# Input projection as a stage of its own, and attention moved beside the blocks that follow it

## The chip, the cores and the metric

The kernel runs on one core of a Trainium2 chip. The metric is the device time of one execution in microseconds. The kernel before takes 2442.66 us (median of 3 runs, 2442.2 to 2445.62). One further execution was profiled. The figures of the profile come from that one.

## The reference

One encoder layer, 512 tokens, width 2048, all in float32:

```python
h  = rmsnorm(x, norm_mix)
qa, ka, va, qb, kb, vb, ga, gb = split(h @ w_in)      # 1024|256|256|1024|1024|1024|2048|2048 columns
qa = rope(rmsnorm(qa)); ka = rope(rmsnorm(ka))        # 8 query heads, 2 key/value heads of 128
out_a = window_attention(qa, ka, va, sink)            # keys within 128 tokens, a sink logit per head
qb = rmsnorm(qb); kb = rmsnorm(kb)                    # 8 heads
out_b = neighbourhood_attention(qb, kb, vb, rpb)      # 8 x 16 window on a grid 64 wide, 2-D bias
merged = sigmoid(ga) * (out_a @ w_branch_a) + sigmoid(gb) * (out_b @ w_branch_b)
x = x + merged @ w_out
u = conv3(rmsnorm(x, norm_ffn) @ w_up) + conv_b       # 2 x 5632 columns, depthwise over tokens
x = x + (silu(gate) * val) @ w_down                   # gate, val = halves of u
```

The input projection `w_in` has 8704 columns: 17 blocks of 512.

## The kernel before

Every matrix product is made in three matmuls: each operand is split into a rounded part `hi` and a rest `lo` (`nc.scalar.copy` to the reduced type, then a subtraction on VectorE), and hi x hi, hi x lo and lo x hi are added up in PSUM. Weights are split in the kernel too, unit by unit, just before use. A unit is two 128-row tiles by 512 columns of a weight (512 KB); a block of `w_in` is 8 units.

A block runs in one of two ways:

- **Plain** (`step` and `run_step`, L120 and L220): four PSUM banks, 16 tiles of the inner dimension, three matmuls of 512 moving columns each, 192 in all. The weights are `Plain` units (their own pool `wst`) or, later on, `Tiles` units (pool `f` for the raw weights, pool `w` for the split ones).
- **As seven products** (`products`, L719): a two-by-two scheme after Strassen and Winograd. Units, activations and results are taken as 2 x 2 blocks of (128 rows, 256 columns); seven block products replace eight. It needs sums of weight blocks (`Product.sums`, three VectorE additions per unit, L632), sums of activations (`form_sums`, `forms`) and, once per block, `combine` (L816), which puts seven PSUM banks together into the result. 8 units x 7 x 2 x 3 = 336 matmuls of 256 moving columns.

For some `Product` units (`kept`) the sums are made long in advance: `make_early` (L680) fetches the weight on the POOL queue, adds (L651, four VectorE additions), stores the sums to DRAM, and the unit later loads them. `windows` says in which units that goes on.

The order of the program up to the branches: `kv_a` (L589) and `q_a` project the rows of branch a, plainly, `v_b` and `kq_b` those of branch b. Each of these steps puts the work that follows on a queue: `rows_of` (norm and rotary of 128 tokens), `head` (transposing a head on TensorE), `run` (one head's attention; `attention_out`, its second half, runs behind the next head). `run_step` takes `rate` entries from that queue per unit, with a raised priority of 400 instructions, so that attention's small matmuls, its VectorE and ScalarE work run between the plain matmuls. Then come the gates: three blocks plainly, five as products (L995 to L1003). `end_attention` (L858) runs what is left in the queue and closes the attention's pools just before the third. While that block runs, `form_h` loads `x` again and makes the forms of `h` for the products. After that `branch` a, `branch` b, the output projection, the up projection with its convolution, and the down projection.

A planner arranges the program of each engine: it simulates the kernel, and takes of the instructions that are ready the one with the highest priority. Instructions marked with `keep`, and every DMA on the SP queue (`dma`, L74), stay in the order in which they were written. Pools are stretches of on-chip memory; a tile over a closed pool waits for the tiles that lay there. `prep_to` splits the weights up to two units ahead, `advance` also loads up to four units ahead.

## Time and profile before

| what | value |
|---|---|
| runs, median (range) | 2442.66 us (2442.2 to 2445.62) |
| profiled execution | 2443.0 us |
| its span, first to last instruction | 2441.2 us, granted clock 0.998 |
| TensorE, VectorE, ScalarE, GpSimd busy | 99%, 77%, 52%, 13% |
| DMA | 517.63 MB in the span, mean 212 GB/s |
| transposes of heads and attention on TensorE | 64.0 to 531.0 us |
| first and last matmul | 5.3 and 2434.1 us |

In the tables of stretches a row gives start and end, the length, then for each engine its busy time and in brackets its instructions, then the granted TensorE clock (1.00 is full speed), the mean busy share of the 16 DMA engines and GB/s. In the groups a row gives line, engine, operation, tiles written and read, shapes, count, then busy time and mean ns of one, then the idle time ahead of them with what ended it. PEld is TensorE's loading of weights, which overlaps its matmuls.

### The profile page before, as it was taken

How to read it: one execution, taken by the hardware profiler on the slowest of the kernel's cores; microseconds unless marked ns; L12 is line 12 of the kernel's file. 1: busy time of each engine (PE TensorE's matmuls, PEld its weight loads, DVE VectorE, ACT ScalarE, POOL GpSimd, SP SyncE). 2: the span in 40 equal slices, each digit the busy share in tenths (PEclk: the TensorE clock that was granted, in tenths of full speed). 3: DMA queues.
4: the chain of work that ended last, by engine and by line, in shares of the span. 5: the costliest groups of instructions: out<-in, count | busy, mean ns of one | idle time of the engine just before them, and what ended most of it. 6: DMA issues, size and time to landing. Idle time of an engine off the chain costs nothing. (4 is left out here: it accounts for less than half of the span.)

```text
span 2441.2 us, 45026 instructions
## 1 busy us (share of the span) xinstructions
PE 2422.1 (99%) x17346; PEld 2264.5 (93%) x17346; DVE 1881.9 (77%) x2911; ACT 1280.2 (52%) x1862; POOL 314.1 (13%) x394
## 2 busy tenths in 40 slices
PE   9999999999999999999999999999999999999998
PEld 7888888888999888888999999999999999999998
DVE  6788676635788657555888888888888877888897
ACT  5254554544545323334566665756667566464643
POOL 1413233100000111110010111101111011000000
PEclk9999999999999999999999999999999999999999
DMA  5677777545455587664577877878778799675953
GB/s 195 243 244 242 255 254 266 174 141 192 169 178 169 194 285 228 237 241 165 161 203 211 221 209 210 219 211 222 208 211 216 213 268 266 172 250 134 315 167 126
DMA packets 300681, 517.63 MB, mean 212 GB/s; under 512 B 26160, under 2 KB 163120, under 8 KB 300464
## 3 DMA queue, kind: packets, MB, share of 16 engines
q1 hardware_dynamic: 217008, 318.18, 40.5%
q0 software_dynamic: 47168, 124.71, 21.0%
q10 hardware_dynamic: 36288, 71.84, 7.8%
q8 instruction: 136, 2.23, 0.4%
q14 instruction: 81, 0.66, 0.1%
HBM read 374.22 MB, written 94.37 MB: 192 GB/s over the span
## 5 line engine op out<-in xcount | busy, mean ns | idle before, releaser
L78 PE MATMUL mm<-s,wh 128*128 128x256 f32 (+1 forms) x9564 | 1689.4, 289 | 6.7 <-ACT wh L674 3.8
L78 PEld LDWEIGHTS mm<-s,wh 128*128 128x128 f32 x9564 | 1400.3, 188 | 48.7 <-ACT wh L674 5.1
L78 PE MATMUL mm<-s,wl 128*128 128x256 f32 (+1 forms) x4782 | 1184.1, 288 | 0.0
L78 PEld LDWEIGHTS mm<-s,wl 128*128 128x128 f32 x4782 | 817.6, 188 | 20.0
L674 ACT CAST wh<-f 128x1024 fp32r<-128x1024 f32 x594 | 547.7, 941 | 517.3 <-PE mm L78 400.1
L675 DVE TENSOR_TENSOR wl<-f,wh 128x1024 fp32r<-128x1024 f32 x594 | 642.8, 1087 | 171.1 <-ACT wh L674 161.6
L632 DVE TENSOR_TENSOR f<-f 128x256 f32<-128x256 f32 (+1 forms) x639 | 325.4, 509 | 7.6 <-DMA f<-in_w_down 2.3
L78 PE MATMUL mm<-hi,s 128*128 128x512 f32 x896 | 286.5, 395 | 5.3 <-ACT hi L162 5.3
L163 DVE TENSOR_TENSOR lo<-raw,hi 128x1024 fp32r<-128x1024 f32 (+1 forms) x97 | 117.7, 1213 | 122.5 <-ACT hi L162 116.8
L78 PEld LDWEIGHTS mm<-hi,s 128*128 128x128 f32 x896 | 168.4, 189 | 38.4 <-ACT hi L162 5.2
L78 PE MATMUL mm<-s,hi 128*128 128x512 f32 x640 | 195.3, 392 | 0.0
L776 DVE TENSOR_TENSOR wl<-f,wh 128x1024 fp32r<-128x1024 f32 x71 | 87.0, 1225 | 134.8 <-ACT wh L775 131.6
L162 ACT CAST hi<-raw 128x1024 fp32r<-128x1024 f32 (+1 forms) x97 | 101.0, 1041 | 155.0 <-PE mm L78 146.5
L775 ACT CAST wh<-f 128x1024 fp32r<-128x1024 f32 x71 | 74.4, 1048 | 199.0 <-PE mm L78 185.4
L78 PE MATMUL mm<-lo,s 128*128 128x512 f32 x448 | 176.1, 394 | 0.0
L78 PEld LDWEIGHTS mm<-s,hi 128*128 128x128 f32 x640 | 119.5, 188 | 23.9
L1072 POOL DMA_DIRECT2D o<-a x44 | 52.9, 1202 | 584.5 <-ACT a L1071 517.6
L78 PE MATMUL mm<-s,lo 128*128 128x512 f32 x320 | 120.4, 392 | 0.0
L651 DVE TENSOR_TENSOR s<-s 128x256 f32<-128x256 f32 x236 | 97.6, 419 | 5.9 <-DMA s<-in_w_in 3.5
L78 PEld LDWEIGHTS mm<-lo,s 128*128 128x128 f32 x448 | 84.8, 189 | 16.1
L1069 ACT ACTIVATE o<-u,smalls 128x512 f32<-128x512 f32 x88 | 71.2, 809 | 18.8 <-ACT wh L674 13.8
L1080 POOL DMA_DIRECT2D o<-a x44 | 52.8, 1201 | 175.5 <-ACT a L1078 161.6
(156 smaller groups left out, 1825.1 us busy)
## 6 DMA issues: line engine op xcount, KB each, us to landing
f<-in_w_up SPq DMA_DIRECT2D x301, 256.0 KB, 3.7
o<-a POOLq DMA_DIRECT2D x88, 511.0 KB, 7.3
f<-sums SPq DMA_DIRECT2D x84, 512.0 KB, 5.6
f<-in_w_down SPq DMA_DIRECT2D x145, 256.0 KB, 4.2
raw<-in_w_in SPq DMA_DIRECT2D x63, 512.0 KB, 3.6
sums<-s ACTq DMA_DIRECT2D x118, 256.0 KB, 2.8
s<-in_w_up POOLq DMA_DIRECT2D x86, 256.0 KB, 5.5
s<-act SPq DMA_DIRECT2D x73, 256.0 KB, 6.1
```

The lines of the kernel that those rows point to most:

```text
L78: return nc.tensor.matmul(o, l, r, start=start, stop=stop, skip_group_check=True).ins
L162: nc.scalar.copy(hi[:, c:c + n], self.raw[:, c:c + n])
L163: nc.vector.tensor_tensor(lo[:, c:c + n], self.raw[:, c:c + n], hi[:, c:c + n].bitcast(F32), ALU.subtract)
L632: add = lambda *args: keep(nc.vector.tensor_tensor(*args, ALU.add))
L651: add = lambda *args: keep(nc.vector.tensor_tensor(*args, ALU.add))
L674: keep(nc.scalar.copy(hi, f))
L675: keep(nc.vector.tensor_tensor(lo, f, hi.bitcast(F32), ALU.subtract))
L775: keep(nc.scalar.copy(hi, self.f))
L776: keep(nc.vector.tensor_tensor(lo, self.f, hi.bitcast(F32), ALU.subtract))
L1069: keep(nc.scalar.activation(self.o[:, m], u[:, m], AF.Identity, bias=cb[:, i:i + 1], scale=cw[:, i, 1:2]))
L1072: keep(nc.gpsimd.dma_start(self.o[:, :, 1:], first[:, :, :S - 1], accum_op=ALU.add))
L1080: keep(nc.gpsimd.dma_start(self.o[:, :, :S - 1], third[:, :, 1:], accum_op=ALU.add))
```

## The change

The input projection of everything but branch b's queries and keys now comes first, without attention beside it:

1. `project_v`, two plain blocks with the values of branch b; their results go to DRAM (`raw_v`). The forms of `h` are made beside the second, from the `x` tiles that are still there.
2. Eight gate blocks and the three blocks of branch a's rows, all eleven as seven products. For the latter the operands are exchanged (`layout="t"`), so that results come out with tokens on partitions; they go to DRAM (`raw_a`).
3. Four plain blocks `project_b` with branch b's queries and keys (their rows go to DRAM too, `raw_b`), and then branch a's projection. All attention is queued in this stage, at 1.85 entries per unit in place of 1.25. Entries that need a raw row (`Loaded`) load it on the SP queue when they are among the first three of the queue. `end_attention` comes ahead of the last unit of branch a's third block.

The stages share on-chip memory: pools are opened and closed at their bounds (`begin_rows`, `begin_attention`, `end_attention`). All units are now `Tiles` or `Product` units with one common loading order (`ready`, `load_units`). The split weights of plain units and of the products' first part stay in one pool (`wa`) throughout. Sums made in advance are now kept for no gate unit, and for one unit of an up block in place of two; the down projection keeps its 17.

The core of the diff ("..." marks what is left out):

```diff
-N_SLOTS, N_P, N_TR, AHEAD = 56, 8, 4, 400
+N_SLOTS, N_EXTRA, N_P, N_TR, N_QR, AHEAD = 56, 8, 8, 4, 7, 400
...
-ATTENTION_RATE, RATE = 1.25, 3
+RATE, ATTENTION_RATE, LOOK = 1, 1.85, 3
...
+    ffn["f"], ffn["bufs"], ffn["width"] = open_("loads", "f1", side="right"), 4, 7
+    ffn["ahead"], ffn["limit"] = 1, -1
+    extra = open_("loads", "extra", side="right")
+    att = {}
+    first_banks = pool("pmm", 4, space=PSUM)
+    more_banks = open_("inner", "pmm1", space=PSUM)
+    banks = {"mm": deque([first_banks] * 4 + [more_banks] * 4)}
 
     def slot(dt=F32):
...
+    def ready(phase, d):
+        while at[phase] < len(units) and at[phase] <= min(at["use"] + d, ffn["limit"]):
+            at[phase] += 1
+            yield units[at[phase] - 1]
+
+    def load_units(d):
+        for u in ready("load", d):
+            u.load()
     def prep_to(n, hooks=((), (), ()), **kw):
...
-            u.prep(*hooks, **kw)
+        for i in range(at["prep"], min(n, ffn["limit"]) + 1):
+            load_units(i - at["use"])
...
     def run_queued(n):
         with tc.high_priority(offset=AHEAD):
             for _ in range(min(n, len(queue))):
+                for work in list(queue)[:LOOK]:
+                    if isinstance(work, Loaded):
+                        work.load()
                 queue.popleft()()
 
...
+    class Loaded:
+
+
+        def __init__(self, load, work, *args):
+            self.start, self.work, self.args, self.tile = load, work, args, None
+
+        def load(self):
+            if self.tile is None:
+                self.tile = self.start()
+
+        def __call__(self):
+            self.load()
+            self.work(self.tile, *self.args)
+
...
+    def load_row(src):
+        raw = att["rows"].tile([P, 4, HD], F32, tag="qr", name="qr", bufs=N_QR)
+        dma(raw.rearrange("p h d -> p (h d)"), src)
+        return raw
...
+        def rows_of(raw, t):
+            if on_row:
+                on_row(t, raw)
+            head_square(raw, nh, t, sums, HD if scaled else 1.0, g is not None)
...
+        queue.extend(Loaded(partial(load_row, src[:, t]), rows_of, t) for t in range(NT))
+        queue.extend(partial(head, h) for h in range(nh))
         return res
...
+    def project_v(half, **kw):
...
+            if m % 2 == 0:
+                held["v"] = quad("u")
+            nc.scalar.copy(held["v"][:, m % 2], ps)
+            if m % 2:
+                nc.gpsimd.dma_start(raw_v[2 * half + m // 2], held["v"])
+
+        step("f", w_in, [(C_VB + half * S, S)], hT, evac, **kw)
+
+    def project_b(pair, **kw):
+
+        def evac(t, ps):
+            o = att["heads"].tile([P, S], F32, tag="o", name="o", bufs=2)
+            nc.scalar.activation(o, ps, AF.Copy, scale=rows["rs"][:, t:t + 1])
+            nc.scalar.dma_start(raw_b[pair][:, t], o)
+
+        step("t", w_in, [(C_QB + pair * 256, 256), (C_KB + pair * 256, 256)], hT, evac,
+             post=lambda: heads_b(pair), rate=ATTENTION_RATE, **kw)
+
+    def heads_b(pair):
+        v = [None] * 2
+
+        def head_v(raw, h):
...
+                nc.tensor.transpose(b[:, i * P:(i + 1) * P], vt[:, k0:k0 + P], ident)
+            v[h] = split(b)
...
+        queue.extend(
+            Loaded(partial(load_row, raw_v[pair][:, h]), head_v, h) for h in range(2))
         res = row_heads(
...
+            raw_b[pair], 4, None,
+            lambda tiles, h: heads_T(tiles, h, part["gqb" if h < 2 else "gkb"], grid=True))
+        queue.extend(partial(run, i) for i in range(2))
+
+    def heads_a():
...
+            split_rows(vh[-1][:, half], vl[-1][:, half],
+                       raw[:, 2:].rearrange("p h d -> p (h d)"), rows["rs"][:, t:t + 1])
+
+        k = row_heads(raw_a[0], 2, "gka", heads_T, on_row=row_v)
+        for half in range(2):
+            scaled = []
+            q = row_heads(raw_a[1 + half], 4, "gqa", heads_T, scaled=scaled)
+
+            def run(i, half=half, q=q, scaled=scaled):
+                behind(attention_a(half * 4 + i, q[i], k, (vh, vl), scaled[0][:, :, i]))
+
+            queue.extend(partial(run, i) for i in range(4))
 
     pending = []
 
...
             added.append((e, u))
-        if early and any(a <= u < b - 4 for a, b in windows) and not (wide and u % 2):
+        if early and any(a <= u < b - 4 and u % n for a, b, n in windows):
...
+                        lh, ll, rh, rl = (
+                            (wh[:, s], wl[:, s], ah, al) if layout == "f" else
+                            (ah[:, s], al[:, s], wh, wl))
+                        mm(o, lh, rh, i == m == 0, False)
+                        mm(o, lh, rl, False, False)
+                        last["pe"] = mm(o, ll, rh, False, i == n - 1 and m == 1)
...
+    def begin_rows():
+
+        opened["loads"].close()
+        ffn["f"], ffn["bufs"], ffn["width"] = open_("rest", "f2", side="right"), 3, 4
+        ffn["ahead"], ffn["limit"] = 3, stage_ends[1]
+        att["tmp"] = open_("rest", "tmp2", side="right")
+        att["rows"] = open_("rest", "rows", side="right")
+        load_masks()
+        prep_to(at["use"] + 1)
+        load_units(2)
+        heads_a()
+
+    def begin_attention():
+
+        opened["inner"].close()
+        del ffn["q"], ffn["b"]
+        tmp["p"], tmp["n"] = att["tmp"], 4
+        att["heads"] = open_("rest", "heads", side="right")
+        att["p"] = open_("rest", "p", side="right")
+        banks["mm"] = deque([first_banks])
+        banks["tr"] = deque([open_("rest", "ptr", space=PSUM)])
+
     def end_attention():
         run_queued(len(queue))
         behind()
...
+        opened["rest"].close()
+        again = lambda name, **kw: ctx.enter_context(
+            tc.tile_pool(name=name, bufs=1, reuse_waits="tile", **kw))
+        ffn["f"], ffn["bufs"], ffn["width"] = again("f3", side="right"), 4, 7
+        ffn["ahead"], ffn["limit"] = 4, len(units) - 1
+        ffn["q"] = again("q3", side="right")
+        ffn["b"] = again("wb3")
+        tmp["p"], tmp["n"] = again("tmp3", side="right"), 3
         del banks["tr"]
...
+        load_units(2)
 
...
+    def form_h(j):
+
+        a, b = xt[2 * j], xt[2 * j + 1]
+        for i, x in enumerate((a, b)):
+            nc.scalar.activation(x, x, AF.Copy, scale=gmix[:, 2 * j + i:2 * j + i + 1])
+        left, right = slice(0, 256), slice(256, 512)
+        add = nc.vector.tensor_tensor
+        add(b[:, right], b[:, right], a[:, right], ALU.subtract)
+        add(a[:, right], a[:, left], a[:, right], ALU.subtract)
+        add(a[:, left], a[:, left], b[:, right], ALU.add)
+        add(b[:, left], a[:, left], b[:, left], ALU.subtract)
+        highs, lows = ((sums_slot(j), sums_slot(j)) for _ in range(2))
+        for hi, lo, x in zip(highs, lows, (a, b)):
+            nc.scalar.copy(hi, x)
+            add(lo, x, hi.bitcast(F32), ALU.subtract)
+        half = lambda k, c: (hT[2 * j + k][0][:, c], hT[2 * j + k][1][:, c])
+        both = lambda i, c: (highs[i][:, c], lows[i][:, c])
+        hf.append([half(0, left), half(1, left), both(1, left), both(0, right),
+                   both(1, right), both(0, left), half(1, right)])
...
+    def row_products(i, c, **kw):
+
+        def evac(*halves):
+            for h, u in enumerate(halves):
+                dst = raw_a[i][:, :, h * 256:(h + 1) * 256].rearrange("p (t m) n -> p m t n", m=2)
+                src = u.rearrange("p m (t n) -> p m t n", t=2)
+                for m in range(2):
+                    nc.gpsimd.dma_start(dst[:, m], src[:, m])
+
+        products(columns(c), range(KD // 2), hf, evac, layout="t", **kw)
 
...
+    def branch_a(blk):
+        def before(kb):
+            if kb == 1:
+                for m in range(4 * blk, 4 * blk + 4):
+                    ra[m] = slot()
+                    nc.gpsimd.dma_start(ra[m], gate_a[m // 2][:, m % 2])
+            if blk == 2 and kb == 3:
+                end_attention()
+            if blk == 3:
+                parts_behind(out_b, ob, 0)(kb)
+
+        def evac(o, ps):
+            m = 4 * blk + o
+            nc.vector.tensor_tensor(ra[m], ps, ra[m], ALU.mult)
+
+        step("f", w_branch_a, [(blk * 512, 512)], oa, evac, nk=8, before=before,
+             rate=ATTENTION_RATE)
+
...
+    project_v(0, pre=first_loads, before=split_hT)
+    project_v(1, before=form_h)
+    for blk in range(8):
+        gate_products(blk)
+    for i, c in enumerate((C_KVA, C_QA, C_QA + 512)):
+        row_products(i, c, after=(
+            lambda u: begin_rows() if u == 7 else None) if i == 2 else None)
+    stage_ends.append(len(units) - 1)
+    windows.append((len(units) + 1, len(units) + 44, 2))
+    for pair in range(4):
+        project_b(pair, pre=begin_attention if pair == 0 else None,
+                  before=parts_behind(out_a, oa, 2) if pair == 3 else None)
     for blk in range(4):
-        branch(w_branch_a, blk, oa, gate_a, evac_a, before=parts_behind(out_b, ob, 0))
+        branch_a(blk)
+    stage_ends.append(len(units) - 5)
+    windows.append((len(units) - 2, len(units) + 48, 3))
     for blk in range(4):
-        branch(w_branch_b, blk, ob, gate_b, evac_b)
+        branch_b(blk)
...
         view = w_up.rearrange("(d b p) (h n) -> d p b h n", b=2, p=P, h=2)
         products(view[:, :, :, :, s * 256:(s + 1) * 256], range(KD // 2), h2, evac,
                  before=before, after=after,
-                 kept={0: range(8), pairs_ff - 1: (2, 3, 7)}.get(s, (2, 3)))
+                 kept={0: range(8), pairs_ff - 1: (2, 3, 7)}.get(s, (2,)))
```

376 lines of the change are left out of this document (120 added, 256 removed).

## The prediction

> **What bounds the kernel now.** I read the page's span and busy lines first, then the waits of TensorE, then stretches of the span in which one kind of work runs alone.
>
> ```profile
> span 2441.2 us, 45026 instructions
> PE 2422.1 (99%) x17346; PEld 2264.5 (93%) x17346; DVE 1881.9 (77%) x2911; ACT 1280.2 (52%) x1862; POOL 314.1 (13%) x394
> ...
> L78 PEld LDWEIGHTS mm<-s,wh 128*128 128x128 f32 x9564 | 1400.3, 188 | 48.7 <-ACT wh L674 5.1
> ...
> PE mm L78 <- ACT hi L162: 5.3, 1, 5.3
> PE mm L78 <- ACT wh L674: 3.8, 1, 3.8
> PE mm L78 <- DVE s L1113: 1.5, 2, 1.2
> PE mm L78 <- ACT s L1112: 1.2, 1, 1.2
> ```
>
> TensorE is busy for 99% of the span and waits for others only 11.8 us in all (last four rows: total, times, longest; the row above them is the weight loads, with busy time and mean ns). 5.3 us of that is the start. A matmul that is gone is therefore worth its full spacing, as long as the other engines keep up. The spacing is read from stretches with one shape only (columns: length, busy time and count of PE, PEld, DVE, ACT, POOL, clock, DMA share, GB/s): branch projections with 512 moving columns in the first row, seven-product blocks with 256 columns in the others (gates, up projection, down projection).
>
> ```profile
> 840.00:1110.00 270.00, 270.00 (x1193) 223.58 (x1192) 158.11 (x249) 80.14 (x104) 34.75 (x62) 1.00 0.72 242
> 680.00:800.00 120.00, 120.00 (x1059) 120.00 (x1058) 99.02 (x136) 60.25 (x72) 3.21 (x6) 1.00 0.53 171
> 1300.00:1900.00 600.00, 599.86 (x5278) 599.47 (x5277) 527.27 (x722) 386.20 (x506) 76.86 (x64) 1.00 0.81 215
> 2300.00:2400.00 100.00, 100.00 (x883) 100.00 (x882) 91.33 (x139) 46.16 (x57) 4.37 (x8) 1.00 0.53 171
> ```
>
> 270/1193 is 0.2263 us for a 512-column matmul, and 120/1059 is 0.1133 us for one of 256. The clock is 1.00 throughout, and no stretch is held back by the DMA engines or VectorE, although VectorE is already at 83, 88 and 91% beside the products.
>
> **The matmuls that go.** A plain 512-column block of the input projection has 4 outputs x 16 tiles x 3 = 192 matmuls: 192 x 0.2263 = 43.4 us. As seven products it has 8 units x 7 x 2 x 3 = 336 of half the width: 336 x 0.1133 = 38.1 us. Five blocks already run as products, and eleven will, so six are converted: 6 x 5.4 = **-32.3 us**. The two `v` blocks and the four `q`/`k` blocks of branch b stay plain, and nothing else is taken from TensorE.
>
> [...]
>
> **VectorE beside the products.** These rows price one unit (busy time, mean ns).
>
> ```profile
> L675 DVE TENSOR_TENSOR wl<-f,wh 128x1024 fp32r<-128x1024 f32 x182 | 222.4, 1222 | 80.0 <-ACT wh L674 80.0
> L675 DVE TENSOR_TENSOR wl<-f,wh 128x768 fp32r<-128x768 f32 x182 | 173.3, 952 | 24.3 <-ACT wh L674 24.3
> L632 DVE TENSOR_TENSOR f<-f 128x256 f32<-128x256 f32 x262 | 110.3, 421 | 3.2
> L632 DVE TENSOR_TENSOR f<-f 128x512 f32<-128x512 f32 x130 | 89.1, 685 | 0.0
> ...
> L823 DVE TENSOR_TENSOR u<-mm,t 128x512 f32<-128x512 f32 x46 | 31.6, 688 | 4.4 <-ACT t L827 2.1 <-DVE t L823 0.5
> L823 DVE TENSOR_TENSOR u<-t,u 128x1024 f32<-128x1024 f32 x23 | 28.0, 1219 | 0.1
> ...
> L845 DVE SCALAR_TENSOR_TENSOR t<-mm,t 128x512 f32<-128x512 f32 x23 | 15.7, 681 | 0.0
> ```
>
> Sums of weights made in advance and kept in DRAM fall, by the lists of kept units in the code, from 84 (16 for gates, 51 for the up and 17 for the down projection) to 48: no gate unit has them and an up block has one in place of two. A unit without them adds 0.685 + 2 x 0.421 = 1.53 us to VectorE. A gate block today spends 0.825 x 38.1 = 31.4 us there with two units kept; with none it is 34.5 of 38.1 us, 91%. An up block goes from 33.5 to 35.0 us, 92%. The down stretch above holds full spacing at 91%, so I cost this at **0**. What hides it is the matmuls of the unit in flight; if nothing above those 91% were usable, an up block would be up to 0.3 us over, +6 in 21 blocks. Below zero it can't go, since those stretches have no stall to give back. The row products have no row factor (1.219 us x 2 less), so they are lighter than the gates. The new `form_h` runs beside the second plain `v` block: 4 x 0.42 + 2 x 0.69 = 3.1 us a unit plus a 1.22 us weight split against 24 x 0.2263 = 5.4 us, so it is covered.
>
> **The seams between stages.** Today plain blocks hand over to products once, at 617 us:
>
> ```profile
> 620.86 3.10 PE L78 MATMUL mm<-s,wh 128*128 128x256 f32 x14 [3.82 <-ACT wh L674]
> ...
> 616.00:636.00 20.00, 16.18 (x122) 15.68 (x121) 17.65 (x30) 13.54 (x25) 3.07 (x5) 0.91 0.67 249
> ```
>
> TensorE stands 3.82 us and then runs at a reduced clock: four wide and 118 narrow matmuls need 14.3 us at full spacing, the stretch took 20, so the seam costs **5.7 us**. The cause is that the weight pool of the plain blocks must close first. In the change that pool (`wa`) is never closed, so this seam should go. A new one appears after the last row product: `begin_rows` may prepare the first unit of `project_b` only after that block's `combine`, whose last VectorE steps need the last matmul: 0.681 + 1.219 us, then the new unit's split of about 1.22 us, 3.1 us in which TensorE has nothing but one matmul. I take the new seam to cost as much as the old one, net **0**, with bounds from -5.7 (it is hidden) to +6 (the old one stays too).
>
> [...]
>
> The second seam is `end_attention` inside branch a's third block: loads of the next block go into tiles over the old `f2`, scratch and mask tiles, so unit 0 of block 3 is loaded one unit ahead and not two. The load takes 3.6 us and the two splits 1.0 and 1.2 (rows below), 5.8 against 5.4 us of cover. I take **+2**, between 0 and +10.
>
> **The attention beside less work.** Attention now runs beside 12 plain blocks. Afterwards it has 43 units of 24 matmuls (four blocks, and branch a up to unit 3 of its third block). Rows: all engines from 50 to 540 us, then in the same stretch VectorE's weight splits (L163), its sums in advance (L651), ScalarE's weight casts (L162) and TensorE's attention instructions, and last the densest 100 us.
>
> ```profile
> 50.00:540.00 490.00, 489.97 (x2456) 415.54 (x2455) 341.17 (x697) 233.08 (x445) 127.86 (x169) 1.00 0.67 223
> ...
> 50.00:540.00 490.00, 90.59 (x74) 1.00 0.67 223
> ...
> 50.00:540.00 490.00, 97.62 (x236) 1.00 0.67 223
> ...
> 50.00:540.00 490.00, 77.75 (x74) 1.00 0.67 223
> ...
> 50.00:540.00 490.00, 100.47 (x672) 91.37 (x672) 76.93 (x138) 55.22 (x91) 1.00 0.67 223
> ...
> 100.00:200.00 100.00, 99.97 (x489) 84.26 (x488) 84.85 (x179) 42.90 (x87) 38.82 (x39) 1.00 0.68 229
> ```
>
> - TensorE: 2456 - 672 = 1784 plain matmuls x 0.2263 = 404 us, so attention itself takes 86 us of it. New stage: 43 x 24 x 0.2263 + 86 = 320 us.
> - VectorE: 341 - 91 - 98 = 153 us for attention, plus 43 splits x 1.22 = 53, plus about 20 sets of sums at 1.65 us (98 us for 236 additions, four a set) = 33 (the window now fetches every second unit), plus 16 splits and evacuations of branch a at 0.69 = 11: 250 of 320 us, 78%.
> - ScalarE: 233 - 78 = 155, plus 43 x 1.05 = 45, plus 5: 205 us, 64%.
>
> From 100 to 200 us VectorE ran at 85% with TensorE at 99.97 busy, so 78% should fit. I cost the crowding at **+3**, nearest to that row. Ends: 0, and, if VectorE can do no more than its mean share of today (341/490 = 70%), 250/0.70 - 320 = +37.
>
> **Raw rows through DRAM.** 36 rows of 256 KB are stored and read back through SP's queue.
>
> ```profile
> raw<-in_w_in SPq DMA_DIRECT2D x63, 512.0 KB, 3.6
> f<-sums SPq DMA_DIRECT2D x84, 512.0 KB, 5.6
> sums<-s ACTq DMA_DIRECT2D x118, 256.0 KB, 2.8
> s<-act SPq DMA_DIRECT2D x73, 256.0 KB, 6.1
> ...
> SPq L75 <- DVE lo L163: 168.7, 32, 10.3
> ```
>
> A row needs about 2.8 us to be stored and up to 6.1 us to come back. A row is asked for two queue entries before its use (`LOOK` 3), two entries are 2/1.85 units, about 6 us, and its store lies far earlier, except in the first unit. Bytes: 36 x 0.5 MB more, but 36 kept sums fewer, each 512 KB fetched, 512 stored and 512 loaded in place of 256. Cost **0**. If the cover goes, a late row delays attention, which the crowding's bound already holds. One wait is new: `project_b` empties its four banks on ScalarE through two `o` tiles, which attention's results use as well, so the third bank waits for the store of the first, some 2.8 us. Behind that copy stand weight casts and attention on ScalarE, and behind the bank the next block's matmuls. The first bank is complete 18 matmuls (4.1 us) before the block's end and the third is wanted 12 matmuls (2.7 us) after it, so the store is covered by 4 us. I take **+1**, between 0 and four times 2.8 us.
>
> **Sum.** 2441.2 - 32.3 + 0 + 0 + 2 + 3 + 0 + 1 = 2414.9 us of span. The profiled execution took 2443.0 us, 1.8 more than its span, and the runs' median of 2442.66 lies 0.3 below it: 2414.9 + 1.8 - 0.3 = **2416 us**. Start, the stall when the down projection begins (L1112, L1113) and the tail are untouched.
>
> **The rivals.**
> - *More than forecast.* The new seam is hidden and nothing crowds: 2416 - 5.7 - 6 = 2404. For it: the stage's VectorE share is only 78%. Against: `combine` is ordered ahead of the new unit.
> - *VectorE sets the attention stage.* Branch a's rotary work comes first and bunches up. At 74%, midway between the mean share and what is needed, 250/0.74 = 338, 18 us over: 2416 - 3 + 18 = 2431. Against it stands the 100 to 200 us row; for it, that this was 100 us and now 320 are wanted.
> - *SP's queue turns on the kernel (slower).* A row load takes one of seven row tiles and waits for it, and each weight load issued later stands behind it. SP's tile waits reach 10.3 us today without touching TensorE, because loads run ahead. With three weight tiles a load is issued two units before its split, 10.9 us less 3.6 of transfer, some 7 us of slack. There are six changes of row group (one `k`/`v`, two `q`, four `b`). If attention runs late by more than the slack, each overshoot stops TensorE. Beyond (32.3 + 4.9)/6, about 6 us each, the kernel is slower by over 0.2%; at 8 us it is 2410 + 48 = 2458 (2410 is the sum without its 6 us of stalls). Against it: rows of a group are freed by its head transposes, and two attention heads are queued after them.
> - *Weight loads set the spacing.* If a narrow matmul had to wait for its own weight load, 188 ns by the first fence, a product block would take 336 x 0.188 = 63 us, 20 over a plain one: 2416 + 32 + 120 = 2568. The loads overlap each other in the product rows (1058 in 120 us), which denies it. [...]
> - *Nothing moves.* Crowding near the end of its range eats the gain: 2410 + 32 = 2442.
>
> **How the numbers follow.** Chances: forecast (2409 to 2422) 0.52; more than forecast 0.12; VectorE sets the stage (2422 to 2437) 0.17; nothing moves 0.07; SP's queue 0.11; weight loads 0.01. A measurement of this kernel tells about 0.2%, 4.9 us, from no change. Faster: 0.52 + 0.12 + 0.17 = 0.81; same 0.07; slower 0.12. The likeliest case's own range is 2409 to 2422. The range for 8 in 10 reaches from 2402 (seam gone, no crowding, 2 us for the clock) to 2440, which takes in the VectorE rival and leaves out the slower ones.
>
> **What would show it.** Right: 6 x 336 = 2016 more narrow matmuls and 6 x 192 = 1152 fewer wide ones, with about 880 in each 100 us of the gate stage; one stall of 3 to 4 us before the first `project_b` matmul, and none at the first gate block; VectorE near 91% beside the gates and 78% in the attention stage. Wrong: TensorE waits spread through the attention stage for weight casts or attention tiles (VectorE rival), or SP waiting on row tiles just before weight loads that TensorE then waits for (SP rival), or clearly fewer than the 5278 matmuls that 600 us of the up projection hold now.

## The result, and the profile after

The changed kernel takes 2517.56 us (median of 4 runs, 2513.09 to 2520.27) against 2442.88 us for the kernel before on the same chip: a ratio of 1.0302, interval 1.0283 to 1.0320. It is 3% slower, where 1% faster was forecast. The profiled execution took 2513.09 us, with a span of 2510.9 us.

The head of the page of the changed kernel:

```profile
span 2510.9 us, 46821 instructions
...
PE 2433.6 (97%) x18210; PEld 2297.7 (92%) x18210; DVE 1995.6 (79%) x3065; ACT 1318.6 (53%) x1883; POOL 270.0 (11%) x334
```

There are 864 matmul records more, as 2016 narrow ones for 1152 wide ones must give. TensorE now stands idle for 77 us of its span (2510.9 - 2433.6); before it was 19. Four stretches of the changed kernel (columns as in the prediction's rows): gates and row products; the attention stage, from the first matmul of `project_b` to the unit behind `end_attention`; branch b with the output projection; the up projection.

```profile
100.00:535.00 435.00, 428.65 (x3700) 426.66 (x3699) 358.81 (x512) 196.69 (x227) 14.58 (x25) 1.00 0.41 134
...
535.40:938.90 403.50, 354.70 (x1721) 291.11 (x1721) 261.27 (x531) 199.17 (x412) 83.97 (x110) 0.95 0.55 183
...
980.00:1300.00 320.00, 320.00 (x1747) 278.15 (x1746) 225.68 (x381) 131.87 (x198) 45.56 (x75) 1.00 0.72 236
1340.00:2040.00 700.00, 696.24 (x6084) 692.71 (x6083) 631.34 (x886) 445.12 (x580) 86.62 (x73) 1.00 0.77 202
```

The attention stage is where the time went: 403.5 us for 44 units, where the prediction's 320 us for 43 units make 325. TensorE is busy for 88% of it at a clock of 0.95, while VectorE is busy for only 65% and ScalarE for 49%. No engine is full.

To place the rest, I compared the time between the starts of successive matmuls with full spacing (0.227 us for 512 columns, 0.175 for 384, 0.113 for 256, 0.108 for a transpose). Full spacing alone fell from 2405.0 to 2371.9 us, by 33.1. What lies above it rose from 23.7 to 126.2 us. A gap is a matmul that starts more than 0.26 us late, a short delay one that starts 0.08 to 0.26 us late:

| stretch of the changed kernel | gaps, us | short delays, us | rest, us |
|---|---|---|---|
| 0 to 100 us, start and `v` blocks | 3.7 | 2.6 | 0.4 |
| 100 to 535, gates and row products | 7.8 (9 gaps) | 1.0 | 6.8 |
| 535 to 980, attention stage | 60.8 (60 gaps) | 24.3 | 0.7 |
| 980 to the end | 10.0 (21 gaps) | 2.9 | 4.6 |

The expectations below call the short delays "lowered clock" or "slow clock". That is true of part of them only: in the attention stage about 13.5 of the 24.3 us lie in the eight stretches, 41 us in all, in which the granted clock was 0.50. The other 11 us came at full clock. Before, attention's stretch (50 to 600 us) had no gap and 7 us of short delays, all at full clock. Of the first 44 units of the changed kernel seven take longer than 9 us, the others 5.4 to 8.8 (number of the unit, its start, its length, from the starts of the plain matmuls in the trace):

```
changed kernel   4 @558 13.2   11 @613 26.2   15 @661 27.7   23 @738 28.6   31 @809 20.2   39 @876 19.0   43 @917 21.9
```

Units 15, 23 and 31 are the last of the second, third and fourth block of `project_b`, which the text below calls blocks 1 to 3. Unit 39 is the last of a branch a block, and at 43 `end_attention` runs what is left of attention. The timeline of unit 23 shows one such end, for TensorE, SP's queue, VectorE and ScalarE in turn (start, length, the instruction, and in brackets the idle time before it with what ended it):

```profile
743.40 0.39 PE L93 MATMUL mm<-wh,s 128*128 128x512 f32 x1
748.90 0.87 PE L549 MATMUL tr<-ident,p 128*128 128x128 f32 x3 [5.12 <-DVE p L581]
...
766.31 0.33 PE L375 MATMUL tr<-ident,qr 128*128 128x128 f32 x1 [0.89 <-ACT o L569]
766.79 0.50 PE L93 MATMUL mm<-wh,s 128*128 128x512 f32 x1 [0.15 <-ACT o L429]
...
721.32 20.32 SPq L90 DMA_DIRECT2D f<-in_w_in  x8
741.74 0.41 SPq L90 DMA_DIRECT2D qr<-raw_v  x1
742.19 0.43 SPq L90 DMA_DIRECT2D bias<-in_bias_b  x1
...
746.33 1.02 DVE L440 TENSOR_TENSOR v<-qr,row 128x512 f32<-128x512 f32 x1 [3.89 <-DMA qr<-raw_v]
...
748.41 1.27 DVE L581 SCALAR_TENSOR_TENSOR p<-tr,bias 128x192 f32<-128x192 f32 x4
...
757.70 0.59 ACT L572 COPY o<-tr 128x512 f32<-128x512 f32 x1 [0.84 <-PE tr L93]
...
765.24 1.02 ACT L569 COPY o<-tr 128x512 f32<-128x512 f32 x1 [1.18 <-PE tr L93]
766.06 0.68 ACT L429 ACTIVATE o<-mm,rs 128x512 f32<-128x512 f32 x1
```

The block's last plain matmul runs at 743.40, the next block's first at 766.79. In between TensorE has only attention's chain, and mostly waits for it. The next block needs an empty bank. The first bank is emptied at 766.06 (L429), behind the results of two attention heads (L572, L569), which use the same two `o` tiles and were written earlier. The tile that L429 needs came free when the store of the first head landed, at 761.49 in the trace; the other 4.6 us it stood behind the second head in ScalarE's order. The heads are late in their turn. VectorE stands for 3.89 us until a row of `v` has landed (L440), and behind it comes the addition of a bias (L581), which ended TensorE's wait of 5.12 us. That row and that bias were asked for only at 741.7 and 742.2 us, because they stand in SP's queue behind eight weight loads, which that queue issued two by two from 721.3 on, as tiles of plain weights came free.

### The profile page after: what moved, and what is told of

It reads as the page before. It is cut to its first block, busy times and chain, and to the rows that moved or that the text cites. A ratio compares the mean times of both kernels' runs of the same rounds, so it can differ in the third digit from the quotient of the medians.

```text
span 2510.9 us, 46821 instructions
## 1 busy us (share of the span) xinstructions
PE 2433.6 (97%) x18210; PEld 2297.7 (92%) x18210; DVE 1995.6 (79%) x3065; ACT 1318.6 (53%) x1883; POOL 270.0 (11%) x334
## 5 line engine op out<-in xcount | busy, mean ns | idle before, releaser
L93 PE MATMUL mm<-s,wh 128*128 128x256 f32 (+1 forms) x10236 | 1845.2, 292 | 23.8 <-ACT wh L785 10.7
L93 PEld LDWEIGHTS mm<-s,wh 128*128 128x128 f32 x10236 | 1510.9, 188 | 82.6 <-ACT wh L672 14.1
L672 ACT CAST wh<-f 128x1024 fp32r<-128x1024 f32 (+1 forms) x690 | 639.1, 942 | 672.0 <-PE mm L93 399.8
L673 DVE TENSOR_TENSOR wl<-f,wh 128x1024 fp32r<-128x1024 f32 (+1 forms) x690 | 747.3, 1086 | 188.2 <-ACT wh L672 182.0
L630 DVE TENSOR_TENSOR f<-f 128x256 f32<-128x256 f32 (+1 forms) x891 | 452.6, 508 | 11.4 <-DMA f<-in_w_down 4.1
L786 DVE TENSOR_TENSOR wl<-f,wh 128x1024 fp32r<-128x1024 f32 (+1 forms) x120 | 145.5, 1213 | 172.0 <-ACT wh L785 168.6
L93 PE MATMUL mm<-wh,s 128*128 128x256 f32 (+1 forms) x1088 | 268.6, 336 | 6.6 <-ACT wh L785 4.6
L785 ACT CAST wh<-f 128x1024 fp32r<-128x1024 f32 (+1 forms) x120 | 124.6, 1039 | 228.3 <-PE mm L93 202.2
L93 PEld LDWEIGHTS mm<-wh,s 128*128 128x128 f32 x1088 | 184.4, 189 | 27.1 <-ACT wh L785 6.0
L93 PE MATMUL mm<-wl,s 128*128 128x256 f32 (+1 forms) x544 | 180.5, 335 | 1.7 <-DVE wl L786 1.5
L93 PEld LDWEIGHTS mm<-wl,s 128*128 128x128 f32 x544 | 102.7, 189 | 13.6 <-DVE wl L786 4.1
L1098 ACT ACTIVATE a<-u,smalls 128x512 f32<-128x512 f32 x88 | 62.4, 709 | 0.0
L1105 ACT ACTIVATE a<-u,smalls 128x512 f32<-128x512 f32 x88 | 58.6, 714 | 7.0 <-DMA o<-a 7.0
```

The source lines that it names most:

```text
L93: return nc.tensor.matmul(o, l, r, start=start, stop=stop, skip_group_check=True).ins
L630: add = lambda *args: keep(nc.vector.tensor_tensor(*args, ALU.add))
L672: keep(nc.scalar.copy(hi, f))
L673: keep(nc.vector.tensor_tensor(lo, f, hi.bitcast(F32), ALU.subtract))
L785: keep(nc.scalar.copy(hi[:, c], self.f[:, c]))
L786: keep(nc.vector.tensor_tensor(lo[:, c], self.f[:, c], hi[:, c].bitcast(F32), ALU.subtract))
```

## The experiments

Four theories came first. K: the casts and splits of plain weights, held to the written order, are late behind attention's work. V: VectorE is late in bursts, from the early sums or from attention's raised priority. R: rows of `q`, `k` and `v` are late in SP's queue. C: 44 plain units are too little cover for attention. Two more came from the timeline above. O: the banks wait for the shared `o` tiles. Q: rows and biases are late, or hold others up, in SP's queue. Runs 1 to 11 are one execution each, runs 12 to 16 medians of 4 to 10. The changed kernel's own four executions lie 7 us apart, so single ones that differ by less are told apart, if at all, by the gaps in their traces.

**Runs 1 to 4: one suspect each.**

```diff
 # run 1, in Tiles.prep, so that attention's stage has no keep here
-            n = 4 // pieces
+            n, hold = 4 // pieces, keep if "q" in ffn else (lambda ins: ins)
...
-                keep(nc.scalar.copy(hi[:, c], self.f[:, c]))
+                hold(nc.scalar.copy(hi[:, c], self.f[:, c]))        # and the split likewise
 # run 2
-    windows.append((len(units) + 1, len(units) + 44, 2))
 # run 3, in load_row
-        dma(raw.rearrange("p h d -> p (h d)"), src)
+        nc.gpsimd.dma_start(raw.rearrange("p h d -> p (h d)"), src)
 # run 4
-N_SLOTS, N_EXTRA, N_P, N_TR, N_QR, AHEAD = 56, 8, 8, 4, 7, 400
+N_SLOTS, N_EXTRA, N_P, N_TR, N_QR, AHEAD = 56, 8, 8, 4, 7, 100
```

> The weight casts and splits of the plain units in the attention stage lose their fixed order (they are `keep` instructions in the changed kernel, behind the sums made in advance and their stores; the kernel before had none there). Theory K, the fixed order holds casts back: TensorE's 61 us of gaps and 24 us of slow clock between 535 and 960 us fall to under a third, time 2517 down to about 2455 to 2465. Theory R, raw rows arrive late behind weight loads on SP: little changes, above 2500. Theory V, VectorE and ScalarE bursts of attention go ahead of the casts by priority: little changes or worse, above 2500. Theory C, too few plain matmuls beside the attention: at most 20 us gained.

> No sums are made in advance during the attention stage (its window is removed; units that then lack kept sums add them in place later). This takes some 33 us of VectorE work, its fetches and its ordered stores out of the stage. Theory K: the fixed order then holds only casts and splits, gaps mostly go, 2450 to 2475 with some loss in the up and down projection. Theory V: about half of the gaps go, 2470 to 2495. Theory R: SP loses its 162 us of waits marked with L649, rows come earlier, 2470 to 2500. Theory C: above 2500.

> Raw rows are loaded from GpSimd's queue in place of SP's, so that they no longer stand behind weight loads that wait for one of three tiles. Theory R: ScalarE's and VectorE's 55 us of waits for raw rows mostly go and with them at least 40 us of the time, 2455 to 2475. Theories K, V and C: under 15 us, above 2500, or slower, since GpSimd's own queue stands up to 69 us behind a memset.

> Attention's lead in priority is 100 instructions in place of 400, about two units. Theory V: weight splits win against late attention more often, gaps fall by half, 2470 to 2490. Theories K and R: under 15 us either way. Theory C: attention slips behind and its rest is run at the end of the stage with nothing beside it, slower than 2517.

Measured: 2512.92, 2510.93, 2513.55 and 2521.89 us. Gaps and short delays in the stage were 84.7, 80.4, 84.7 and 94.2 us, against 85.1. None of these edits alone gives back more than 7 us of the 75 that were lost. In run 3 the rows left SP's queue but were not early: ScalarE still waits 23.9 us for them, in place of 41.8. And VectorE now waits for biases, which stayed in SP's queue; in the changed kernel no such wait shows. First two rows of ScalarE's waits in the changed kernel (total, times, longest), then the two rows in run 3, then VectorE's for biases there:

```profile
ACT t L346 <- DMA qr<-raw_b: 21.2, 7, 7.8
ACT qr L344 <- DMA qr<-raw_a: 20.6, 5, 5.6
```

```profile
ACT qr L344 <- DMA qr<-raw_a: 13.9, 5, 3.7
...
ACT t L346 <- DMA qr<-raw_b: 10.0, 5, 4.6
```

```profile
DVE p L581 <- DMA bias<-in_bias_b: 7.0, 3, 4.2
```

**Runs 5 to 8: the two couplings, apart and together.**

```diff
 # run 5 (O), in project_b
-            o = att["heads"].tile([P, S], F32, tag="o", name="o", bufs=2)
+            o = slot()
 # run 6 (Q), in load_row and attention_b
-        dma(raw.rearrange("p h d -> p (h d)"), src)
+        nc.gpsimd.dma_start(raw.rearrange("p h d -> p (h d)"), src)
-        dma(bias, bias_b[:, h * 640:(h + 1) * 640])
+        nc.gpsimd.dma_start(bias, bias_b[:, h * 640:(h + 1) * 640])
 # run 7: both. Run 8: both, and the edit of run 2
```

> The evacuation of the four plain blocks gets slots of its own and no longer the two o tiles of attention's results. Theory O (the banks of a finished block wait for the attention heads that were written before, because their results take the same two tiles, and TensorE is left with attention's serial chain for some 20 us at the ends of blocks 1, 2 and 3): 35 to 60 us come back, 2458 to 2483 us, and the gaps and the lowered clock of the stage fall from 85 to under 50 us. Theory Q (in SP's queue, row and bias loads that wait for a free tile hold up the weight loads written behind them): under 12 us, over 2503. Theory C (44 plain units are too little cover for attention's chains, however tiles and queues are laid out): under 12 us, over 2503.

> Row loads and bias loads are issued by GpSimd's queue and not by SP's; the o tiles stay shared. Theory Q: 35 to 60 us come back, 2458 to 2483 us. Theory O: under 15 us, over 2500, and the stalls at the ends of blocks 1 to 3 stay near 20 us each. Theory C: under 10 us, over 2505. With only the rows moved, 4 us came back, so under Q it is the bias loads, two tiles of 320 KB, that block.

> Own slots for the evacuation, and rows and bias by GpSimd's queue. If O and Q each hold a part, neither edit alone gives much and both together give 50 to 80 us: 2437 to 2467 us, gaps and lowered clock in the stage under 30 us. If O alone holds: as with own slots alone, within 8 us. If Q alone holds: as with the queue alone, within 8 us. Theory C: over 2500.

> As the run before it (own slots, rows and bias by GpSimd), and without the early sums in the attention stage, whose loads and stores share GpSimd's and ScalarE's queues. Alone their removal gave 7 us. Under O and Q, with the coupling gone, VectorE's load matters little: within 6 us of the run before it. If VectorE's bursts (theory V) are what is left: 10 to 25 us below it.

Measured: 2493.97, 2494.57, 2474.22 and 2472.28 us. The two edits give 23.6 and 23.0 us alone and 43.3 together: O and Q each hold, side by side, each at less than I expected of it alone. Together they stay short of the 50 to 80 us expected, and run 7 keeps 45.9 us of gaps and short delays in the stage, not under 30. Run 8 is 2 us below run 7, so the 10 to 25 us that theory V asked of the early sums aren't there. The stage in run 7:

```profile
537.50:899.60 362.10, 337.47 (x1721) 283.58 (x1720) 258.43 (x529) 198.81 (x410) 100.20 (x142) 0.97 0.60 199
```

It holds the 1721 matmuls of before in 362.1 us instead of 403.5. VectorE's work is nearly the same, so the 41 us came back without any less of it. The long units show what each edit did:

```
run 5 (own slots)   4 @560 13.3   11 @615 29.0   17 @679 9.6   18 @689 20.8   26 @756 20.2   31 @801 15.8   39 @858 20.4   43 @896 24.6
run 6 (own queue)   5 @568 11.2   10 @607 11.2   11 @618 29.6   15 @669 20.5   16 @690 10.2   23 @743 16.8   31 @802 17.7   32 @820 13.6   43 @903 14.6
run 8 (both)        7 @578  9.3   10 @602 12.6   11 @614 29.4   15 @665 9.7   18 @688 16.3   26 @752 13.1   31 @789 14.8   35 @824  9.1   43 @883 11.4
```

With own slots the stalls at the ends of blocks 1 and 2 (units 15, 23) are gone, and two stalls appear inside blocks (18, 26). With its own queue the stalls at the block ends stay and are shorter, and that of unit 39 is gone. Unit 11 stays at 26 to 30 us in all of them: neither edit touches it, and in run 8 the waits there are mostly for casts and splits of attention's own tiles. A long unit isn't all loss, as attention's own matmuls run in it. Biases were never moved without rows; that 4 us came from the rows alone and 23 from both is all that is known of their shares. How late the rows are doesn't tell what they cost: in run 7 ScalarE still waits 31.0 us for them (L344, L346).

**Runs 9 and 10: more plain work beside attention.** Two gate blocks become plain blocks between those of `project_b`, in run 9 on top of run 8, in run 10 on the changed kernel as it was.

```diff
+    plain_gates = {0: 6, 1: 7}
...
+    def gate_plain(blk):
+        dst = (gate_a, gate_b)[blk // 4]
+
+        def evac(o, ps):
+            m, t = 4 * (blk % 4) + o, slot()
+            nc.vector.tensor_tensor(t, ps, rows["m"], ALU.mult)
+            nc.scalar.activation(t, t, AF.Sigmoid)
+            nc.gpsimd.dma_start(dst[m // 2][:, m % 2], t)
+
+        step("f", w_in, [(C_GA + blk * 512, 512)], hT, evac, rate=ATTENTION_RATE)
...
+        if pair in plain_gates:
+            gate_plain(plain_gates[pair])
...
-RATE, ATTENTION_RATE, LOOK = 1, 1.85, 3
+RATE, ATTENTION_RATE, LOOK = 1, 1.36, 3
```

> The run with own slots, rows and bias by GpSimd and no early sums in the stage (2472.3 us, gaps and lowered clock 43 us there), with two of the eight gate blocks put back as plain blocks between the first three of project_b, and the rate of attention lowered from 1.85 to 1.36 steps a unit to fit 60 units. Each block put back costs 192 x 0.2263 - 336 x 0.1133 = 5.4 us of matmuls. Theory C (what is left is too little plain work beside attention's chains): the 43 us fall to 10 to 25, 2448 to 2466 us. If what is left is the order in which the heads are written, however much plain work stands beside them: 2478 to 2486 us.

> The changed kernel with the same two gate blocks as plain blocks and the rate of 1.36, its tiles and queues untouched. Theory C as the larger cause: the 85 us of gaps and lowered clock in the stage fall to 40 to 60, 2483 to 2505 us. Theories O and Q as the larger causes: each block end and each late bias load stalls as before, at two more block ends, 2515 to 2535 us.

Measured: 2461.91 and 2519.76 us. First the stage of run 9, then that of run 10, 60 units each:

```profile
456.90:883.90 427.00, 415.65 (x2104) 351.80 (x2104) 255.88 (x471) 223.11 (x437) 83.10 (x111) 1.00 0.45 144
```

```profile
458.80:944.10 485.30, 442.82 (x2105) 367.89 (x2105) 288.15 (x555) 225.64 (x440) 88.77 (x118) 0.94 0.53 173
```

With the couplings gone, cover counts: gaps and short delays fall from 43.0 to 23.2 us, and the run is 10.4 us faster although it has 10.8 us of matmuls more. With them in place the same cover is worth next to nothing (85.1 to 80.3 us). Why it can't help there was not taken apart: of nine units longer than 9 us in run 10 only two (15 and 23) end a block in front of branch a, so stalls at every block end, as expected, are not the reason. C holds, but only behind O and Q, and cover was changed together with attention's rate, so their shares are not known.

**Run 11: the boundaries of the product blocks.** The gates' row factor is left out, and an up block again has two units with sums made in advance.

```diff
-            queue.extend((row_factor_on, store))
+            queue.append(store)
...
-                 kept={0: range(8), pairs_ff - 1: (2, 3, 7)}.get(s, (2,)))
+                 kept={0: range(8), pairs_ff - 1: (2, 3, 7)}.get(s, (2, 3)))
```

> The changed kernel with two edits in stages far apart, read stage by stage. The gates' row factor is left out (two VectorE instructions of 1.22 us a block; the gates are then sigmoids of unscaled rows), and the up blocks have units 2 and 3 made in advance again, not 2 alone. Theory B (at a product block's boundary VectorE is late by a burst of combine and row factor, which the kept sums used to make room for): the gaps of 100 to 535 us fall from 7.8 to under 2, those after 980 us from 10.0 to under 6, and the time to 2503 to 2509 us. If the boundary waits for banks or for ScalarE instead: the gaps stay, over 2512 us.

Measured: 2512.5 us, above the range of theory B and at the edge of its rival's. But the attention stage had 91 us of gaps and short delays in this run, 6 more than in the changed kernel, and the rival wanted the gaps to stay. Stage by stage theory B holds, for the gates less fully than expected: their gaps fall from 7.8 to 3.3 us, not under 2, and the up blocks' (1330 to 2050 us) from 6.7 to 0.8. The burst is seen in the timelines of VectorE, ScalarE and TensorE at a gate boundary of the changed kernel:

```profile
185.52 0.42 DVE L630 TENSOR_TENSOR f<-f 128x256 f32<-128x256 f32 x1
185.85 1.22 DVE L833 TENSOR_TENSOR u<-t,u 128x1024 f32<-128x1024 f32 x1
186.99 2.35 DVE L946 TENSOR_TENSOR u<-u,row 128x1024 f32<-128x1024 f32 x2
189.26 0.41 DVE L630 TENSOR_TENSOR f<-f 128x256 f32<-128x256 f32 x1
...
189.78 0.83 ACT L672 CAST wh<-f 128x768 fp32r<-128x768 f32 x1 [6.07 <-DVE f L630]
...
190.67 0.97 PE L93 MATMUL mm<-s,wh 128*128 128x256 f32 x6 [0.73 <-ACT wh L672]
```

Between two sums of the next unit's weights (L630, at 185.52 and 189.26) stand 3.4 us of `combine` and row factor. The cast that needs the second one comes at 189.78 after 6.07 us of idling, and TensorE's next matmul starts about 0.9 us late. TensorE's waits from 100 to 535 us, changed kernel and run 11:

```profile
PE mm L93 <- ACT wh L672: 6.2, 8, 1.1
```

```profile
PE mm L93 <- ACT wh L672: 1.4, 7, 0.2
```

**Runs 12 to 16: what is left, and whether it can be won back.** Run 12 is run 9 with the row factor two queue entries later (nothing left out) and two kept units per up block. Run 13 has a third gate block put back at a rate of 1.1, and run 14 is run 13 with the edit of run 1. Run 15 is run 12 with the edit of run 1 and early sums in the stage again; run 16 starts those sums in two units of three, at a rate of 1.28.

```diff
 # run 12
-            queue.extend((row_factor_on, store))
+            queue.extend((later, later, row_factor_on, store))   # later does nothing
 # run 15; run 16 with 3 for 2
+    windows.append((len(units) + 1, len(units) + 60, 2))
```

> The run with own slots, rows and bias by GpSimd, no early sums in the stage and two gate blocks put back (2461.9 us), with the gates' row factor computed two units later than now (nothing left out) and units 2 and 3 of an up block made in advance again. Theory B: leaving the row factor out took 4.5 us of gaps from the gates and the second kept unit 5.9 us from the up blocks; six gate blocks are left, so 3 + 6 = 9 us: 2451 to 2455 us, gaps of 100 to 460 us under 4. If a later row factor only moves the burst: 2455 to 2458 us.

> As the run before it with a third gate block put back and the rate at 1.1. A block costs 5.4 us of matmuls. Theory C: the 23 us of gaps and lowered clock left in the stage fall to 10 to 14, so the time stays within 6 us of the run before it, 2446 to 2455 us. If the rest of the loss is a matter of the first heads' order and of the seams at both ends of the stage: 4 to 7 us above the run before it. No theory has it below 2440.

> As the run with three gate blocks put back, and the casts and splits of the plain units' weights are no longer held to the written order. Theory K (kept order delays the casts behind attention's work), which gave 4.6 us on the changed kernel itself where other waits came first: 4 to 10 us below the run with three blocks. If the order of the casts never mattered: within 3 us of it.

> The mended run with two gate blocks put back (2455.1 us), with early sums made in the attention stage again and the casts of plain weights not held to the written order. In the mended run the up blocks still had 9.2 us of gaps although units 2 and 3 are listed, since the sums that the stage used to make in advance were missing. If the sums, not the list alone, are what the up blocks lack: their gaps fall to 1 to 3 us, 6 to 8 us of the time; the unkept casts give 4 to 7 us as with three blocks; the sums cost the stage 2 to 5: 2443 to 2450 us. If the sums crowd the stage as much as they help the up blocks: 2450 to 2455 us.

> As the run before it with early sums started in two units of three rather than one of two, and attention's rate at 1.28. More sums for the up blocks and steps of attention further apart: within 4 us of the run before it if the stage no longer depends on small changes of the written order; 5 to 15 us above it if attention's end is pushed into the seam at the third block of branch a.

| run | median, us | ratio to before, interval | gaps and short delays in the stage, us |
|---|---|---|---|
| 12 | 2455.10 | 1.0055, 1.0040 to 1.0070 | 21.5 |
| 13 | 2463.00 | 1.0084, 1.0069 to 1.0099 | 23.3 |
| 14 | 2456.15 | 1.0058, 1.0041 to 1.0074 | 18.0 |
| 15 | 2444.76 | 1.0010, 1.0000 to 1.0019 | 20.8 |
| 16 | 2448.33 | 1.0027, 1.0016 to 1.0038 | 26.7 |

Against run 9 the gates' gaps fell in run 12 from 8.0 to 2.0 us, but those from 1300 to 2050 us, the up blocks and the stall behind them, stayed (9.1 and 9.2): a list of kept units helps only if their sums have been made, and the stage no longer made any. In run 15 it does: the gaps there are 4.0 us, not quite the 1 to 3 expected, and 620 us of the up projection (run 12 first) hold 77 matmuls more:

```profile
1340.00:1960.00 620.00, 616.18 (x5378) 613.21 (x5377) 560.46 (x790) 392.37 (x513) 76.87 (x64) 1.00 0.76 200
```

```profile
1340.00:1960.00 620.00, 619.87 (x5455) 619.53 (x5455) 546.37 (x748) 398.98 (x522) 78.51 (x66) 1.00 0.81 214
```

The third gate block (run 13) cost 7.9 us and freed nothing in the stage, a little beyond the 4 to 7 of the rival that cover is used up. Unkept casts (run 14), which gave 4.6 us on the changed kernel, within its spread, gave 6.9 us once the other waits were gone: theory K holds for a small part. Run 15 comes within 0.1% of the kernel before: its matmuls need 2382.9 us, 22 less than before, and 46 us lie above that in place of 24. No run's median was below the kernel before. Run 16 is 3.6 us above run 15, within the 4 expected of a stage that no longer depends on small changes of the written order; but its stage has 6 us more of gaps and short delays, so that question stays open. What makes up the some 20 us left there was not taken apart further; in run 15 one block end (656 to 681 us) and the seam at `end_attention` hold about two thirds of it.

## Why the prediction was wrong

- *The matmuls that go, -32.3 us.* Right: full spacing fell by 33.1 us. The weight loads did not set the spacing: 2557 matmuls went through in the 300 us of gates from 100 us on, 0.117 us each with the gaps.
- *The `o` tiles, +1.* This step failed, and it is the clearest case. It saw that `project_b`'s banks share two tiles with attention's results, and priced the wait as one store, 2.8 us, covered by 4. But tiles are handed out in the written order, so the first bank waits for the heads written before it, not only for its own block's stores. The timeline above has 23 us between two plain matmuls at such an end, where the range stopped at 11 for all of them; the edit of one line gave back 23.6 us.
- *Rows through DRAM, 0.* Failed. The cover was counted in queue entries (6 us), but a load is issued when SP's queue comes to it, and there it stands behind weight loads that are paced by TensorE. ScalarE waited 41.8 us for rows in the two rows quoted. Moving rows and biases to another queue gave 23.0 us. Of the SP rival the place was right and the direction, as far as the traces tell, wrong: it feared rows holding up weight loads, but no weight cast of the stage waits for its load, and rows and a bias were held up. Biases, which share that queue, were not counted at all.
- *Attention beside less work, +3.* Failed in kind. The busy times themselves were right (VectorE 250 us forecast and 261 measured, ScalarE 205 and 199), but it took room for a fit. Attention is a chain from engine to engine; with too little plain work behind it TensorE waits although nobody is full. Its waits were spread over attention's tiles, which the prediction had listed as the sign of the VectorE rival, yet VectorE was at 65%. The bound of +37 was made of VectorE's share as well. Run 9 against run 8 puts 20 us on it, with the couplings gone.
- *VectorE beside the products, 0.* The averages were high (forecast 91% beside the gates and 92% beside the up blocks; measured 85% from 100 to 400 us and 631.34/700 = 90%), so there was room on average; the zero failed because it took the average for every place in a block. The upper bound, 0.3 us an up block and +6 in all, came close to the 6.7 measured. The gates' 7.8 us were missed: a stretch that is 85% full on average can be late by 3.4 us of other work at one place in each block. That the sums made in advance had made room there is shown for the up blocks (run 11), for the gates it is argued.
- *Seams, 0 and +2.* The old seam is gone and the new one in front of `project_b` hardly shows: its longest wait between 530 and 541 us is 0.34 us, where 3.1 were forecast. That is some 5 us better than the net 0 assumed. The start lost 3 to 4 us (two waits of 1.37 and 1.62 us around the row factor), which no step had. At `end_attention` TensorE waits 2.55 us and then loses some 1.6 to a slower clock (the last fence), 4 us against +2 and inside its range.
- *The sum.* 96 us lie between the forecast span (2414.9) and the measured one. About 74 of them are in the attention stage: 86 above full spacing, of which 6 were there before and 6 were forecast. Some 15 are in the gates and row products, 9 in the up projection and 4 at the start; the seam gives some 5 back. The range's lower end, 2402, counts 2 us for the clock, which no run shows: at the new seam the clock stayed at 1.00 (530 to 545 us), and behind the wait at `end_attention` a slower clock took some 1.6 us. The range and the rivals had single mechanisms with single prices. None had several waits that feed each other: a late row makes a head late, a late head keeps a bank full, a full bank takes the plain work away that should have hidden the head. The timeline of unit 23 shows this once; over the whole stage the gains of the two edits nearly add up, so how much the waits feed each other is not measured.

## What to carry to other kernels

When work that is hidden beside a stream of matmuls shares a rotating tile or an in-order queue with that stream, each shared item ties the two together in the written order, as the `o` tiles and SP's queue did here (23.6 and 23.0 us); look up who holds the tile before you price the wait by the last store. Busy shares say whether work fits, not whether a chain of it is hidden (VectorE was busy for 65% of the attention stage and ScalarE for 49%, and TensorE had 60.8 us of gaps there): count how much independent work stands beside each chain, and take the couplings away first, because extra cover was worth next to nothing while they were there (run 10) and 10 us net when they were gone (run 9).

## What the hardware showed that was not expected

Eight times in the attention stage the clock fell to 0.50 beside a short wait of TensorE, so that such waits cost more than their length. At `end_attention` it waits from 936.3 to 938.9 us:

```profile
938.89 1.65 PE L93 MATMUL mm<-s,wh 128*128 128x512 f32 x3 [2.55 <-ACT wh L785]
```

The clock before that wait, behind it, and when it has recovered:

```profile
930.00:935.00 5.00, 3.93 (x24) 2.73 (x22) 1.64 (x3) 3.63 (x8) 0.00 (x0) 1.00 0.73 287
939.00:943.00 4.00, 4.00 (x11) 3.19 (x12) 2.23 (x2) 0.79 (x1) 3.29 (x5) 0.60 0.94 293
943.00:946.00 3.00, 3.00 (x15) 2.46 (x14) 0.00 (x0) 0.05 (x1) 0.00 (x0) 1.00 0.93 287
```

The mean granted clock over those 4 us is 0.60; the trace has it at 0.50 for 3.4 us from 938.8 on and at 1.00 again behind that. The stage has eight such stretches of 3.4 or 6.8 us, and about 13.5 us of short delays lie in them. Each begins during a wait of at least 1.6 us or within 1.9 us of its end. Not every such wait has one: behind 2.16 us (to 639.0) the clock stayed at 1.00. At seven of the eight that wait was of 1.6 to 2.6 us, shorter than the 3.1 us that the prediction expected at the new seam, where the longest was 0.34 us and the clock stayed at 1.00. At the eighth it was 5.12 us (to 748.9); in the kernel before, behind the 3.82 us at the old seam, the trace has one stretch of 3.4 us at 0.50. Six of the eight stretches have several waits in the 8 us ahead of them, two (at 747.6 and 856.9) only one, so the runs don't settle what decides, beside the wait itself, whether the clock falls.
